# Seven down products of a SwiGLU layer, spread in another order over four tiles, with each product's weight sum fetched a tile earlier

## The chip, the cores and the metric

The program runs on one core of a Trainium2 chip. That core has a matrix engine (TensorE; PE in the profile, its weight loads PEld), a vector engine (VectorE, DVE), an activation engine (ScalarE, ACT), GpSimd (POOL) and a queue that issues transfers (SyncE, SP). Each engine runs its own list of instructions in order and waits on semaphores for the others. The metric is the device time of one launch in microseconds, as the median of several runs.

## The reference

One decoder layer on 512 tokens of width 1024: a SwiGLU block, a mixer (dilated attention and a gated recurrence), and a second SwiGLU block, each between RMS norms, all in float32:

```python
def swiglu(x, w_gate, w_up, w_down):
    return (jax.nn.silu(x @ w_gate) * (x @ w_up)) @ w_down

f = swiglu(rms_norm(h, ffn1_norm_pre), ffn1_w_gate, ffn1_w_up, ffn1_w_down)
h = h + 0.5 * rms_norm(f, ffn1_norm_post)
...  # the mixer
f = swiglu(rms_norm(h, ffn2_norm_pre), ffn2_w_gate, ffn2_w_up, ffn2_w_down)
h = h + 0.5 * rms_norm(f, ffn2_norm_post)
```

The hidden width is 2816, that is 22 tiles of 128. The change touches the two SwiGLU blocks alone ("first part" in its short description is the first group of four tiles of each block).

## The kernel before

**Number format.** A float32 operand is split into a high part (rounded by ACT, `split`, L260) and a low part (what is left, by DVE, L261); a product is three matmuls: high by high, high by low, low by high. "The form" of something below is this pair. Its high part is made on ACT, its low part on DVE, and TensorE needs both.

**One SwiGLU block** (`ffn`). Tiles 0 to 3 are computed by plain products (`gemm`, `std_out`). Tiles 4 to 21 go through `prod(f, w)`: gate and up of one tile as seven products p1 to p7 (a 2x2 split of the matrices) in place of eight. `w_forms` (L556) makes the seven weight forms of the next tile out of one 1 MB transfer (`raw`): sums on DVE, then four splits. Inside `prod` three results are copied out of PSUM in the middle of the tile: after p1 to a second bank (L793), after p5 (`copy`, L781) and after p6 (`copy`, L781). p6 and p7 accumulate onto the bank that was just copied, so TensorE can't start p6 before the copy after p1 and can't start p7 before the copy after p6.

**Down.** Tiles 0 to 15 are multiplied by the down matrix in four groups a = 0 to 3 of four tiles each, again as seven products, here called steps p1, p2, p5, p6, p7, p3, p4 (`step`, L735 to L760). A step is twelve matmuls of 128x512 (two token blocks of 128, two rows of the group, three matmuls each). It goes to one of two pairs of PSUM banks: p1, p6, p7 and p4 to `db` (banks 3 and 4), p2, p5 and p3 to `dz` (banks 6 and 7); a result that accumulates is read out to `facc` after every step (L756 by ACT, L758 and L760 by DVE). Tiles 16 to 21 are done at the end of the block by `last_product`.

**What a step needs.** (1) The forms of the activations, seven per group, made out of the four tiles' results in `ub` by `first_forms` (p1, p5) and `other_forms` (p2, p3, p6, p7, p4); they lie in `act`, one slot for each of the seven. (2) The form of its weight sum, in one of two buffers `wd0` and `wd1` used in turn: the form of a step can be made only when the step two before it is through. (3) The weight sum itself. The sums are made by transfers that add: in `npair` (`home.x`) u0 + u1 is the sum of p5, adding g0 makes that of p6, adding g1 that of p3; in `dr0` g0 is that of p1, and u0 + g0, loaded anew, that of p7; in `dr1` g1 is that of p2 and u1, loaded anew, that of p4. All these transfers stand in POOL's queue, in order. Adding to `npair` can start only when the form of the step before was read from it.

**The order before.** `ffn_order` puts a window of steps behind each `prod(f)`: in a steady group (p1, p2), (p5, p6), (p7, p3), (p4). `supply(a, p)` makes the form of a step and issues the next load; it is called for the step two ahead, with `tc.high_priority(offset=AHEAD)`. So p5 and p6 fall into one tile, and the form of p6 there waits for a transfer that can start only when the form of p5 is made. The final order on each engine is made by a scheduler out of program order, priorities and estimated durations, not by the program text alone.

```python
WINDOWS = (("p1", "p2"), ("p5", "p6"), ("p7", "p3"), ("p4",))
FIRST_WINDOWS = ((), ("p1", "p2"), ("p5", "p6"), ("p7", "p3", "p4"))
```

## Time and profile before

| | |
|---|---|
| median of 3 runs | 1268.39 us (1267.67 to 1268.49) |
| profiled execution | 1268.15 us, of which the span of the instructions is 1266.4 us |
| mean granted TensorE clock | 0.989 |
| busy: PE, PEld, DVE, ACT, POOL | 97%, 88%, 78%, 56%, 6% of the span |
| first SwiGLU block with its start | about 0 to 345 us |
| second SwiGLU block | from about 925 us on |

In the timeline a row is: start and duration in microseconds, engine, line and operation, result <- operands, and in brackets how long the engine had stood idle before it and what released it. In the windows view a row is a stretch of the span: its length, then each engine's busy time with its count of instructions, the granted TensorE clock (1.00 is full speed), the share of time the transfer engines were busy, and GB/s. In the waits view a row is: engine and line that waited <- engine and line it waited for: microseconds in total, times, longest.

### The profile page before, as it was taken

The numbers are of one execution on the slowest core, as the hardware profiler recorded it, in microseconds if no ns is written. First come the engines' busy times: TensorE is split into PE (matmuls) and PEld (weight loads), VectorE is DVE, ScalarE is ACT, GpSimd is POOL, SyncE is SP. The second block draws the span as 40 slices with busy tenths as digits, with TensorE's granted clock in tenths as the row PEclk, the third lists the DMA queues.
The fourth block names the chain that finished last, engine by engine and source line by source line (L and its number), as shares of the span: only waits on it lengthen the run. The fifth ranks groups of instructions, "written<-read, shape, count | busy, mean of one in ns | idle before, by whom it ended". The sixth has DMA issues, their size and how long they took to land. (4 is left out here: it accounts for less than half of the span.)

```text
span 1266.4 us, 19105 instructions
## 1 busy us (share of the span) xinstructions
PE 1228.6 (97%) x7652; PEld 1110.0 (88%) x7652; DVE 987.4 (78%) x1549; ACT 704.1 (56%) x1159; POOL 75.9 (6%) x123
## 2 busy tenths in 40 slices
PE   9899999989999999999999999999999999999997
PEld 7789898989977899999988787888899889898996
DVE  7989898988577488898665878655789788888855
ACT  7556454544455456656545978734656545555442
POOL 1001110100102000000000000000110111010000
PEclk9999999999999999999999999999999999999999
DMA  8246554543634222232242221325552555455241
GB/s 288 89 113 181 134 167 116 167 117 101 233 117 145 80 100 76 78 107 69 99 168 98 100 100 67 127 84 207 155 176 100 148 128 160 122 167 128 78 172 67
DMA packets 35449, 162.36 MB, mean 128 GB/s; under 512 B 3872, under 2 KB 7072, under 8 KB 23328
## 3 DMA queue, kind: packets, MB, share of 16 engines
q1 hardware_dynamic: 17712, 106.08, 23.0%
q0 software_dynamic: 17648, 55.06, 17.3%
q8 instruction: 60, 0.98, 0.3%
q14 instruction: 29, 0.24, 0.1%
HBM read 150.64 MB, written 6.29 MB: 124 GB/s over the span
## 5 line engine op out<-in xcount | busy, mean ns | idle before, releaser
L261 DVE TENSOR_TENSOR w<-raw,w 128x1024 fp32r<-128x1024 f32 (+1 forms) x241 | 257.8, 1073 | 88.7 <-ACT w L260 84.5
L260 ACT ACTIVATE w<-raw 128x1024 fp32r<-128x1024 f32 (+1 forms) x241 | 224.9, 938 | 132.2 <-PE bank L277 47.2
L774 PE MATMUL bank<-big,w 128*128 128x256 f32 x864 | 251.1, 291 | 21.1 <-ACT c L781 16.1
L776 PE MATMUL bank<-big,w 128*128 128x256 f32 x864 | 248.5, 288 | 1.5 <-DVE w L261 1.5
L775 PE MATMUL bank<-big,w 128*128 128x256 f32 x864 | 248.4, 288 | 0.0
L774 PEld LDWEIGHTS bank<-big,w 128*128 128x128 f32 x864 | 169.9, 197 | 26.9 <-ACT c L781 18.1
L776 PEld LDWEIGHTS bank<-big,w 128*128 128x128 f32 x864 | 169.6, 196 | 2.0 <-DVE w L261 1.9
L775 PEld LDWEIGHTS bank<-big,w 128*128 128x128 f32 x864 | 169.9, 197 | 1.4
L586 PE MATMUL bank<-big,w 128*128 128x256 f32 x320 | 92.0, 288 | 0.0
L587 PE MATMUL bank<-big,w 128*128 128x256 f32 x320 | 91.8, 287 | 0.0
L588 PE MATMUL bank<-big,w 128*128 128x256 f32 x320 | 91.0, 284 | 0.0
L745 PE MATMUL bank<-wd,act 128*128 128x512 f32 x224 | 87.7, 392 | 0.0
L744 PE MATMUL bank<-wd,act 128*128 128x512 f32 x224 | 87.1, 391 | 0.0
L746 PE MATMUL bank<-wd,act 128*128 128x512 f32 x224 | 87.0, 390 | 0.0
L261 DVE TENSOR_TENSOR w<-s,w 128x1024 fp32r<-128x1024 f32 x52 | 63.6, 1223 | 15.4 <-ACT w L260 15.2
L275 PE MATMUL bank<-big,w 128*128 128x512 f32 x192 | 74.8, 389 | 0.0
L277 PE MATMUL bank<-big,w 128*128 128x512 f32 x192 | 74.8, 389 | 0.0
L276 PE MATMUL bank<-big,w 128*128 128x512 f32 x192 | 74.7, 389 | 0.0
L586 PEld LDWEIGHTS bank<-big,w 128*128 128x128 f32 x320 | 61.3, 191 | 1.1
L587 PEld LDWEIGHTS bank<-big,w 128*128 128x128 f32 x320 | 61.3, 192 | 0.0
L588 PEld LDWEIGHTS bank<-big,w 128*128 128x128 f32 x320 | 61.3, 192 | 0.0
L260 ACT ACTIVATE w<-s 128x1024 fp32r<-128x1024 f32 x52 | 54.8, 1054 | 8.1 <-PE bank L588 5.4
(332 smaller groups left out, 2969.3 us busy)
## 6 DMA issues: line engine op xcount, KB each, us to landing
raw<-in_w SPq DMA_DIRECT2D x94, 1024.0 KB, 4.8
dr<-in_wdn POOLq DMA_DIRECT2D x40, 512.0 KB, 4.4
npair<-in_wdn POOLq DMA_DIRECT2D x32, 512.0 KB, 5.5
big<-act POOLq DMA_DIRECT2D x6, 512.0 KB, 4.6
h<-in_x SPq DMA_DIRECT2D x8, 256.0 KB, 6.0
h<-in_xn POOLq DMA_DIRECT2D x4, 512.0 KB, 5.5
kept_m<-h POOLq DMA_DIRECT2D x4, 512.0 KB, 2.9
h<-kept_m POOLq DMA_DIRECT2D x4, 512.0 KB, 4.8
```

The costliest lines, as they stand in the source:

```text
L260: ACT.activation(dh, src, AF.Copy)
L261: DVE.tensor_sub(dl, src, dh.bitcast(F32))
L275: PE.matmul(ps, wh, xh, start=first, stop=False)
L586: PE.matmul(ps, wh, xh, start=start and k == 0, stop=False, skip_group_check=True)
L587: PE.matmul(ps, wh, xl, start=False, stop=False, skip_group_check=True)
L588: PE.matmul(ps, wl, xh, start=False, stop=k == 3, skip_group_check=True)
L744: PE.matmul(ps, xh, wh, start=start and k == 0, stop=False, skip_group_check=True)
L745: PE.matmul(ps, xh, wl, start=False, stop=False, skip_group_check=True)
L746: PE.matmul(ps, xl, wh, start=False, stop=k == 1, skip_group_check=True)
L774: PE.matmul(ps, wh, xh, start=start and k == 0, stop=False, skip_group_check=True)
L775: PE.matmul(ps, wh, xl, start=False, stop=False, skip_group_check=True)
L776: PE.matmul(ps, wl, xh, start=False, stop=k == 3, skip_group_check=True)
```

## The change

- The windows are the same for all four groups: (p1, p2), (p5), (p6, p7), (p3, p4), and start one tile later: group a begins after tile 5 + 4a where it began after tile 4 + 4a (5 for the first group).
- The form of a step is no longer made two steps ahead by `supply` with raised priority, but inside `prod`, between its p2 and p7, for the steps that follow that tile. `down_form` then issues the transfer of the next step that uses the same tile of sums (`NEXT`).
- The activation forms are made in three portions, at tiles with f % 4 equal to 2 (p1, p5), 3 (p2, p6, p7, and the sum for p4) and 0 (p3, p4). Tile 4's result goes to a temporary, and ACT copies it to `ub` after the first group's forms.
- The first loads of a block (`begin`) no longer start as soon as the queue reaches them: two one-element DVE copies out of tile 1's result into `dr0` and `dr1` hold them back until that result exists; the loads of p5 follow after tile 3.
- The slots of `act` for tiles 16 to 21 and the spare room move by one tile.

```diff
-WINDOWS = (("p1", "p2"), ("p5", "p6"), ("p7", "p3"), ("p4",))
-FIRST_WINDOWS = ((), ("p1", "p2"), ("p5", "p6"), ("p7", "p3", "p4"))
+WINDOWS = (("p1", "p2"), ("p5",), ("p6", "p7"), ("p3", "p4"))
...
-        if f // 4 <= SEVEN:
-            a = f // 4 - 1
-            order.append(("window", a, (FIRST_WINDOWS if a == 0 else WINDOWS)[f % 4]))
+        a, i = divmod(f - NSTD - 1, 4)
+        if 0 <= a < SEVEN:
+            order.append(("window", a, WINDOWS[i]))
...
+        def second_forms():
             act_form("p2", x10)
+            DVE.tensor_sub(x01, x11, x01)
+            DVE.scalar_tensor_tensor(x00, x11, -1.0, x00, op0=ALU.mult, op1=ALU.subtract)
+            act_form("p6", x00)
+            act_form("p7", x01)
+
+        def third_forms():
+            DVE.scalar_tensor_tensor(x10, x00, -1.0, x10, op0=ALU.mult, op1=ALU.subtract)
+
+        def fourth_forms():
             act_form("p3", x11)
...
             act_form("p4", x10)
...
+        def supply(a, p):
+
+            if p in ("p5", "p6", "p3"):
+                dst, qs = home.x, {"p5": ("u0", "u1"), "p6": ("g0",), "p3": ("g1",)}[p]
+            else:
+                dst, qs = dr[p in ("p2", "p4")], {"p1": ("g0",), "p2": ("g1",), "p7": ("u0", "g0"), "p4": ("u1",)}[p]
+            for i, q in enumerate(qs):
+                load(dst, a, q, i > 0 or p in ("p6", "p3"))
+            at[p] = dst
+
+        NEXT = {"p1": "p7", "p2": "p4", "p5": "p6", "p6": "p3", "p7": "p1", "p3": "p5", "p4": "p2"}
+
+        def down_form(a, p):
             w = wdt[home.n % 2]
             home.n += 1
-            split(w[:, 0, :], w[:, 1, :], src)
+            split(w[:, 0, :], w[:, 1, :], at[p])
             ready[p] = w
-
-        def supply(a, p):
-
-            with tc.high_priority(offset=AHEAD):
...
+            q = NEXT[p]
+            a += p in ("p7", "p3", "p4")
+            if a < SEVEN:
+                supply(a, q)
+
+        def begin():
+            for i in range(2):
+                DVE.tensor_copy(dr[i][:, 0:1], ub[:, 1, 0:1])
+            for p in ("p1", "p2"):
+                supply(0, p)
...
-            u = ub[:, f % 4, :] if f < LAST[0] else tmp("u")
+            u = ub[:, f % 4, :] if NSTD < f < LAST[0] else tmp("u")
...
+            for a, p in due:
+                down_form(a, p)
             product("p7", b, False)
...
-            elif f % 4 == (2 if f < 8 else 1):
+                if f == LAST[0]:
+                    fourth_forms()
+            elif f % 4 == 2:
                 first_forms()
             elif f % 4 == 3:
-                other_forms()
+                second_forms()
+                third_forms()
+            elif f % 4 == 0 and f > NSTD:
+                fourth_forms()
...
+                if j == 1:
+                    begin()
                 if j + 1 == NSTD:
+                    supply(0, "p5")
...
-                u = prod(ev[1], forms.pop(ev[1]))
+                due = order[i + 1]
+                u = prod(ev[1], forms.pop(ev[1]), [(due[1], p) for p in due[2]] if due[0] == "window" else [])
                 if ev[1] == NSTD:
-                    for _ in range(2):
-                        supply(*todo.pop(0))
+                    first_forms()
+                    second_forms()
+                    third_forms()
+                    fourth_forms()
+                    ACT.activation(ub[:, 0, :], u, AF.Copy)
...
                     step(ev[1], p)
-                    if todo:
-                        supply(*todo.pop(0))
```

The counts of matmuls, splits and transfers stay as they are; two DVE copies of 128x1 and one ACT copy of 128x512 per block are added.

More of the change, by code (lines that the diff above doesn't have):

```diff
@@ L624, in __init__ @@
             self.x = npair.rearrange("p k t -> p (k t)")
-            self.n = 0
+            self.n = self.m = 0
         def slot(self, i):
@@ L637, in room @@
         def room(self):
-            return self.act[:, 12:16, :].rearrange("p (s k) t -> p s (k t)", s=2)
+            return self.act[:, 10:14, :].rearrange("p (s k) t -> p s (k t)", s=2)
         def gain_rows(self):
@@ L668, in ffn @@
         lo_, hi_ = HALVES
+        x00, x01, x10, x11 = ub[:, 0:2, lo_], ub[:, 0:2, hi_], ub[:, 2:4, lo_], ub[:, 2:4, hi_]
         def first_forms():
-            x00, x01 = ub[:, 0:2, lo_], ub[:, 0:2, hi_]
             act_form("p1", x00)
@@ L674, in first_forms @@
             act_form("p5", x00)
-        def other_forms():
-            d1, x01, x10, x11 = ub[:, 0:2, lo_], ub[:, 0:2, hi_], ub[:, 2:4, lo_], ub[:, 2:4, hi_]
+        def second_forms():
             act_form("p2", x10)
-            act_form("p3", x11)
-            DVE.tensor_sub(x01, x11, x01)
-            DVE.scalar_tensor_tensor(x11, x11, -1.0, d1, op0=ALU.mult, op1=ALU.subtract)
-            act_form("p6", x11)
-            act_form("p7", x01)
-            DVE.scalar_tensor_tensor(x10, x11, -1.0, x10, op0=ALU.mult, op1=ALU.subtract)
+            DVE.tensor_sub(x01, x11, x01)
[5 more added lines that the diff above has]
+        def fourth_forms():
+            act_form("p3", x11)
             act_form("p4", x10)
         def last_act(f):
-            v = home.slot(f - LAST[0])
+            v = home.slot((f - LAST[0] - 1) % 8)
             return v[:, 0, :], v[:, 1, :]
@@ L698, in load @@
                 nc.gpsimd.dma_start(dst, stored(a, q))
-        ready = {}
-        def down_form(p, src):
+        ready, at = {}, {}
+        def supply(a, p):
[8 more added lines that the diff above has]
+        def down_form(a, p):
             w = wdt[home.n % 2]
             home.n += 1
-            split(w[:, 0, :], w[:, 1, :], src)
+            split(w[:, 0, :], w[:, 1, :], at[p])
             ready[p] = w
-        def supply(a, p):
-            with tc.high_priority(offset=AHEAD):
-                if p == "p1":
-                    load(dr[0], a, "g0")
-                    down_form(p, dr[0])
-                    load(home.x, a, "u0")
-                    load(home.x, a, "u1", True)
-                elif p == "p2":
-                    load(dr[1], a, "g1")
-                    down_form(p, dr[1])
-                elif p == "p5":
-                    down_form(p, home.x)
-                    load(home.x, a, "g0", True)
-                    load(dr[0], a, "u0")
-                    load(dr[0], a, "g0", True)
-                elif p == "p6":
-                    down_form(p, home.x)
-                    load(home.x, a, "g1", True)
-                elif p == "p7":
-                    down_form(p, dr[0])
-                    load(dr[1], a, "u1")
-                elif p == "p3":
-                    down_form(p, home.x)
-                else:
-                    down_form(p, dr[1])
+            q = NEXT[p]
[7 more added lines that the diff above has]
+                supply(0, p)
         def step(a, p):
@@ L760, in step, with prod @@
                         DVE.tensor_add(y, ps, y)
-        def prod(f, w):
+        def prod(f, w, due):
             g = tmp("g")
             b, y, z = b_of[f % 2][:, :HB], y_[:, :HB], z_[:, :HB]
-            u = ub[:, f % 4, :] if f < LAST[0] else tmp("u")
+            u = ub[:, f % 4, :] if NSTD < f < LAST[0] else tmp("u")
             def product(p, ps, start):
@@ L817, in finish @@
                 split(*last_act(f), u)
-            elif f % 4 == (2 if f < 8 else 1):
+                if f == LAST[0]:
+                    fourth_forms()
+            elif f % 4 == 2:
                 first_forms()
             elif f % 4 == 3:
-                other_forms()
+                second_forms()
+                third_forms()
+            elif f % 4 == 0 and f > NSTD:
+                fourth_forms()
         keys = [(w, n, i) for i in range(NSTD) for w in ("gate", "up")]
         forms = {}
-        todo = [(a, p) for a in range(SEVEN) for p in STEPS]
-        for ev in ffn_order(n):
+        order = ffn_order(n)
+        for i, ev in enumerate(order):
             if ev[0] == "std":
@@ L834, in ffn @@
                     steps[j]()
+                if j == 1:
+                    begin()
                 if j + 1 == NSTD:
+                    supply(0, "p5")
                     for f in steps[NSTD:]:
                         f()
-                    first_forms()
-                    other_forms()
             elif ev[0] == "prep":
```

## The prediction

> **What bounds the kernel now.** First the page's busy line.

> ```profile
> span 1266.4 us, 19105 instructions
> PE 1228.6 (97%) x7652; PEld 1110.0 (88%) x7652; DVE 987.4 (78%) x1549; ACT 704.1 (56%) x1159; POOL 75.9 (6%) x123
> ```

> TensorE is busy for 1228.6 of 1266.4 us, and the change leaves its matmuls as they are. So it can gain only from the 37.8 us in which PE stands idle, or from stretches in which PE runs at a lower clock; it can lose by new idle time. Second, the waits view, for PE.

> ```profile
> PE bank L774 <- ACT c L781: 16.1, 7, 3.8
> PE bank L774 <- ACT big L260: 3.2, 1, 3.2
> ```

> The first entry is a product in `prod` that waits for ACT's copy `c`. Third, the timeline of PE, for where these waits lie.

> ```profile
> 57.68 0.39 PE L776 MATMUL bank<-big,w 128*128 128x256 f32 x1 [1.10 <-DVE w L261]
> 62.37 0.80 PE L774 MATMUL bank<-big,w 128*128 128x256 f32 x2 [3.23 <-ACT big L260]
> 95.67 0.38 PE L774 MATMUL bank<-big,w 128*128 128x256 f32 x1 [1.49 <-ACT c L781]
> 145.78 0.57 PE L774 MATMUL bank<-big,w 128*128 128x256 f32 x1 [2.02 <-ACT c L781]
> 209.31 0.39 PE L774 MATMUL bank<-big,w 128*128 128x256 f32 x1 [2.18 <-ACT c L781]
> 274.44 0.39 PE L774 MATMUL bank<-big,w 128*128 128x256 f32 x1 [3.77 <-ACT c L781]
> 989.71 0.39 PE L774 MATMUL bank<-big,w 128*128 128x256 f32 x1 [0.98 <-DVE ub L786]
> 1039.80 0.38 PE L774 MATMUL bank<-big,w 128*128 128x256 f32 x1 [2.37 <-ACT c L781]
> 1103.30 0.38 PE L774 MATMUL bank<-big,w 128*128 128x256 f32 x1 [2.15 <-ACT c L781]
> 1165.24 0.39 PE L774 MATMUL bank<-big,w 128*128 128x256 f32 x1 [2.07 <-ACT c L781]
> ```

> Six stalls of 2.0 to 3.8 us come once per group of four tiles, in groups 1 to 3 of both blocks; the 1.49 at 95.67 is the first group's. Their cause, around 209.31, in the timeline of ACT, DVE and POOL:

> ```profile
> 198.70 1.06 ACT L260 ACTIVATE wd<-npair 128x1024 fp32r<-128x1024 f32 x1 [1.64 <-PE bank L746]
> 200.67 1.22 DVE L261 TENSOR_TENSOR wd<-npair,wd 128x1024 fp32r<-128x1024 f32 x1
> 202.30 0.89 POOL L696 DMA_DIRECT2D npair<-in_wdn  x1 [13.10 <-DVE wd L261]
> 207.93 1.06 ACT L260 ACTIVATE wd<-npair 128x1024 fp32r<-128x1024 f32 x1 [3.26 <-DMA npair<-in_wdn]
> 208.90 0.37 ACT L781 ACTIVATE c<-bank 128x256 f32<-128x256 f32 x1
> ```

> p5's form is made at 198.70 and its low part on DVE at 200.67; only then POOL starts the transfer that adds to `npair`, and ACT stands 3.26 us before p6's form until it has landed. The copy `c` that frees p7's bank stands behind that form: it runs at 208.90, and PE goes on at 209.31. From form to form it takes 207.93 - 198.70 = 9.2 us, and one tile isn't long enough for both.

> Fourth, the windows view, by stretches from stall to stall and just behind two stalls; it shows the clock.

> ```profile
> 60.50:67.30 6.80, 4.93 (x23) 4.94 (x24) 5.87 (x7) 2.21 (x3) 0.86 (x2) 0.50 0.66 231
> 145.78:149.20 3.42, 3.42 (x16) 3.42 (x17) 2.62 (x4) 2.11 (x3) 0.87 (x1) 0.51 0.15 13
> 210.68:214.10 3.42, 3.42 (x18) 3.42 (x17) 2.59 (x4) 0.75 (x1) 0.86 (x1) 0.50 0.54 83
> 145.78:209.31 63.53, 61.35 (x420) 57.60 (x420) 55.83 (x81) 32.54 (x51) 6.24 (x9) 0.97 0.51 141
> 209.31:274.44 65.13, 61.35 (x421) 57.61 (x421) 56.49 (x82) 33.07 (x52) 6.20 (x9) 0.97 0.50 138
> 274.44:345.00 70.56, 70.56 (x477) 66.14 (x478) 50.69 (x70) 34.23 (x53) 5.50 (x9) 0.98 0.49 158
> 1039.80:1103.30 63.50, 61.35 (x420) 57.60 (x420) 55.84 (x81) 32.55 (x51) 6.19 (x9) 0.97 0.51 141
> 1103.30:1165.24 61.94, 59.87 (x421) 56.12 (x421) 56.32 (x82) 33.07 (x52) 6.22 (x9) 1.00 0.52 145
> 1165.24:1225.00 59.76, 59.76 (x427) 57.07 (x428) 44.84 (x62) 29.51 (x46) 3.54 (x6) 0.97 0.36 115
> ```

> The granted clock falls to half (0.50, 0.51) for 3.42 us behind the stalls of 2.02 and 2.18 us. Half of such a window is lost, 1.7 us. The whole stretches say where it happened: 0.97 of 63.5 us is 1.9 us short of full, so one window each; only 1103.30:1165.24 has 1.00. PE's work shows it too: about 420 matmuls took 61.35 us in the stretches with a window and 59.87 in the one without. So five of the six stalls bring a half-clock window. The stall of 3.23 at 62.37 lies in two (6.80 us at 0.50).

> [...]

> **The change, part by part.** The sum is made against the profiled execution (1268.15 us, span 1266.4), 0.24 under the median of 1268.39; I leave this difference aside.

> *p5 and p6 in different tiles.* In a steady group each form of `wd` is now made outside the stretch between the three copies: p5's early in the tile with f % 4 = 2, p6's at that tile's end, 8 to 9 us later (an estimate from the order of ACT's instructions with the durations above). The 9.2 us from form to form are just about there; if the transfer is late by a us, p6's form delays no copy that PE needs soon, as p6's first matmul follows only behind the next tile's products, some 10 us on or more (four tiles take 60 to 65 us in the rows above). p7, p3, p4, p1 and p2 have a tile or more each, and the additions still stand in POOL's queue in the order of their use. So all six stalls go: 2.02 + 2.18 + 3.77 + 2.37 + 2.15 + 2.07 = 14.56 us. With them go five windows of half clock: 5 x 1.7 = 8.5 us.

> *What is late next.* The cover of every step is DVE, which needs 55.8 to 56.5 us per four tiles; PE without stall and window needs 63.53 - 2.18 - 1.7 = 59.65. So DVE fits with 3 us to spare, less than it has now: between 1103.30 and 1165.24 it stood idle for 61.94 - 56.32 = 5.62 us. I cost it at nothing, since no instruction is added for it and what PE waited for was ACT; without the cover each us that it is late costs one per group.

> *Two steps behind one tile.* In (p1, p2), (p6, p7) and (p3, p4), ACT has a second form and a form of activations ahead of the copy out of the bank (L793). Now:

> ```profile
> 47.54 0.63 ACT L260 ACTIVATE act<-ub 128x512 fp32r<-128x512 f32 x1 [0.94 <-PE bank L277]
> ...
> 174.39 0.37 ACT L793 ACTIVATE bank<-bank 128x256 f32<-128x256 f32 x1 [0.39 <-PE bank L776]
> 175.77 0.38 ACT L781 ACTIVATE c<-bank 128x256 f32<-128x256 f32 x1 [1.01 <-PE bank L776]
> ```

> ACT stood 0.39 idle before that copy; a form of 0.63 ahead of it makes the copy 0.24 later. PE reaches the next copy's product 175.77 - 174.39 = 1.38 us on, less 0.37 for the copy: 1.0 us of slack, so it is hidden. p6 and p7 share banks 3 and 4, so the second begins only when the first was read out. I take 0.05 us in each of eight groups, 0.4; the bounds are 0 and the 0.3 per group of one read-out, 2.4.

> *The start of the first block.* The forms of p1 and p2 were made by 23.48, the second's start; the delayed loads put them behind `tx` on ACT, at 48.08:

> ```profile
> 23.48 1.05 ACT L260 ACTIVATE wd<-dr 128x1024 fp32r<-128x1024 f32 x1
> 42.98 1.22 DVE L472 TENSOR_TENSOR t<-h 128x1024 f32<-128x1024 f32 x1
> 48.08 1.05 ACT L260 ACTIVATE tx<-t 128x1024 fp32r<-128x1024 f32 x1
> 50.57 1.06 ACT L260 ACTIVATE big<-h 128x1024 fp32r<-128x1024 f32 x1 [1.45 <-DVE h L490]
> 52.43 1.06 ACT L260 ACTIVATE w<-s 128x1024 fp32r<-128x1024 f32 x1
> 53.52 1.23 DVE L261 TENSOR_TENSOR w<-s,w 128x1024 fp32r<-128x1024 f32 x1
> dr<-in_wdn POOLq DMA_DIRECT2D x40, 512.0 KB, 4.4
> ```

> The small DVE copies stand right behind the row at 42.98, so the loads start at about 44.5 and land 4.4 us later, at 49, the second at 50 (an estimate). Two forms are 2 x 1.06 = 2.1 us on ACT; 1.45 us of idle stand before 50.57, so `w` at 52.43 is 0.6 to 0.8 us later, and DVE's 53.52 with it. DVE has no idle time from there to the stall at 62.37, which grows by 0.8 (from 0, if the loads land early, to 2.1).

> The two stalls of the first group other than the 1.49 are these, in PE's timeline:

> ```profile
> 82.85 0.39 PE L776 MATMUL bank<-big,w 128*128 128x256 f32 x1 [0.39 <-DVE w L261]
> 85.58 0.39 PE L774 MATMUL bank<-big,w 128*128 128x256 f32 x1 [0.30 <-DVE ub L786]
> ```

> The first group is now drawn into four tiles like the others but its activation forms come only after tile 4, so p5's low form stands behind weight sums: I take the wait at 95.67 as 2.1 in place of 1.49 (+0.6), 0.9 for sums that DVE makes later, 0.7 for the copy behind the forms, and 0.7 off for these 0.39 and 0.30, which go with the order that made them. A stall of 2.1 also brings a window, +1.7. Together 0.8 + 0.6 + 0.9 + 0.7 - 0.7 + 1.7 = 4.0; bounds 0 (none comes) and 9 (the two forms in full, and 3.77, the largest stall there is, with its window on top of the present ones).

> *The second block's start.* ACT and DVE have idle time there, so the forms cost nothing. p6's form no longer stands ahead of the sums at 989.71: 0.98 becomes about 0.6, -0.4 (0 to -1). The copy of 128x512 (0.63 by the form of that size) and the small DVE copies are hidden, as is the moved spare room.

> Sum: -14.6 - 8.5 - 0.4 + 0.4 + 4.0 = -19.1. From 1268.15 that is 1249.0 us.

> **The rivals.**

> *DVE becomes the bound (slower).* The 5.6 us idle per group is time in which DVE waited in order for ACT's high parts and can't be worked off. Then four tiles go on taking about 62 to 65 us whatever ACT copies, the stalls only move from `c` to DVE's `w`, and the start's 4.0 is lost: 1272. It decides from 4 us of idle per group on, where 56.3 + 5.6 exceeds 59.65 by the 2.3 that a stall now costs. Against it: the stretch 274.44 to 345.00 has no stall with the same engines, and much of the present idle is caused by the stall itself.

> *The half clock isn't these stalls'.* If four of the five windows come from something else than the 2 us stalls, only the 3.77's window goes, and a new stall of 2.1 brings none: -14.6 - 1.7 - 0.4 + 0.4 + 2.3 gives 1254.1. Against it: 0.50 in 210.68:214.10, right behind a 2.18 stall. [...]

> *The copy out of the bank is late.* If the forms delay L793 by 0.7 us more than its slack in 14 tiles with two steps: +9.8, about 1259. Against it: 1.0 us of slack against 0.24.

> *The first block's start costs its upper bound:* up to +9, so 1253 to 1254, to 1260 if weights of the first group are late as well. For it: DVE has no idle time there.

> *It doesn't do what it says:* p6's form still waits between the copies, about 1268. Against it: in the built order it stands behind the tile's last copy.

> **How the numbers follow.** Main case (1243 to 1253) 0.64; better than 1243, with no cost at the start and shorter waits elsewhere, 0.03; clock rival 0.07; late copy 0.07; heavy start 0.07; no change 0.03; DVE bound 0.09. The time is the main case's, 1249.0. From 1242 to 1260 hold the main case, the clock, the copy and the start, 0.85; the start's bounds of 0 and +9 alone make 1245 to 1254. About 0.2% (2.5 us) is what a measurement tells from no change: faster 0.88, same 0.03, slower 0.09.

> **What would show it.** In the changed kernel's waits, PE behind ACT's `c` falls from 16.1 us to about 2, all at the first group; stretches of four tiles last 59.7 to 60.5 us at a clock of 1.00; the stall at 62 is 4.0 and the one at 57.68 1.1 to 1.9; p6's form waits for its transfer without PE waiting. It would be wrong if PE waits for DVE's `w` or `act` forms once a tile, for L793's copy, or if 0.50 stays without stalls.

## The result and the profile after

The changed kernel takes 1281.33 us (median of four runs, 1277.50 to 1282.36) against 1268.03 for the kernel before: a ratio of 1.0112, with a 95% interval of 1.0072 to 1.0152. It is slower by 1.1%, where 1249.0 was forecast with 1242 to 1260 as the range. The kernel before was run again beside every experiment, and moved by some tenths of a per cent from one set of runs to the next (medians of 1262.05 to 1268.39), so what follows goes by ratios.

The profiled execution of the changed kernel took 1281.76 us. First its page, the span and the busy line:

```profile
span 1280.0 us, 19095 instructions
PE 1234.2 (96%) x7652; PEld 1112.6 (87%) x7652; DVE 986.1 (77%) x1553; ACT 705.4 (55%) x1161; POOL 75.6 (6%) x123
```

The span grew by 13.6 us. PE stands idle for 45.8 us in place of 37.8, which is 8.0 of it; the other 5.6 are busy time of the same 7652 matmuls, that is, a lower clock (a mean of 0.984 where it was 0.989). Second, the waits of PE (who waited <- for whom: us, times, longest):

```profile
PE bank L772 <- ACT bank L791: 11.2, 6, 2.7
PE bank L772 <- DVE ub L784: 8.0, 5, 3.4
PE bank L772 <- DVE u L784: 3.6, 2, 2.1
PE bank L772 <- ACT big L259: 3.2, 1, 3.2
```

L772, L779, L784 and L791 are the lines 774, 781, 786 and 793 of before. The copy `c`, 16.1 us before, is no longer at the head: its stalls in the later groups are gone, as forecast. In their place stand 11.2 us behind the copy out of the bank (L791) and 11.6 behind the sums (L784), which had 1.8 before. In PE's timeline:

```profile
60.26 0.79 PE L772 MATMUL bank<-big,w 128*128 128x256 f32 x2 [3.24 <-ACT big L259]
114.14 1.22 PE L742 MATMUL bank<-wd,act 128*128 128x512 f32 x2 [2.63 <-ACT wd L259]
172.84 0.39 PE L772 MATMUL bank<-big,w 128*128 128x256 f32 x1 [0.97 <-DVE ub L784]
200.70 0.39 PE L772 MATMUL bank<-tx,w 128*128 128x256 f32 x1 [2.48 <-ACT bank L791]
238.30 0.39 PE L772 MATMUL bank<-big,w 128*128 128x256 f32 x1 [1.22 <-DVE ub L784]
265.55 0.38 PE L772 MATMUL bank<-tx,w 128*128 128x256 f32 x1 [1.75 <-ACT bank L791]
303.07 0.39 PE L772 MATMUL bank<-big,w 128*128 128x256 f32 x1 [1.53 <-DVE u L784]
...
1045.12 0.44 PE L772 MATMUL bank<-big,w 128*128 128x256 f32 x1 [3.40 <-DVE ub L784]
```

Two stalls come again and again. One is at the boundary of two groups, where p1's and p2's forms are made, ahead of groups 2 and 3: 2.48 and 1.75 here, 2.47 and 1.42 in the second block, 8.1 us together. The other follows p6's form, in groups 1, 2 and 3: 0.97, 1.22 and 1.53 here, 1.23, 1.22 and 2.06 in the second block, 8.2 us together.

**The stall at the boundary.** The timelines of ACT, DVE and POOL up to 200.70, in order of time:

```profile
180.27 1.04 ACT L259 ACTIVATE wd<-dr 128x1024 fp32r<-128x1024 f32 x1
183.58 1.22 DVE L260 TENSOR_TENSOR wd<-npair,wd 128x1024 fp32r<-128x1024 f32 x1
185.47 0.55 POOL L701 DMA_DIRECT2D npair<-in_wdn  x1 [14.06 <-ACT c L779]
189.06 1.22 DVE L260 TENSOR_TENSOR wd<-dr,wd 128x1024 fp32r<-128x1024 f32 x1
189.58 0.90 POOL L699 DMA_DIRECT2D npair<-in_wdn  x1 [3.57 <-DMA npair<-in_wdn]
190.89 0.55 POOL L701 DMA_DIRECT2D dr<-in_wdn  x1 [0.41 <-DVE ub L810]
199.32 1.06 ACT L259 ACTIVATE wd<-dr 128x1024 fp32r<-128x1024 f32 x1 [3.53 <-DMA dr<-in_wdn]
200.28 0.37 ACT L791 ACTIVATE bank<-bank 128x256 f32<-128x256 f32 x1
```

p3's form has its low part at 183.58, p4's only at 189.06, though ACT made its high part at 180.27. p5's two loads follow p3's form (185.47, 189.58), and the load of p2's sum follows p4's (190.89), behind them in the queue. It is used about a tile later, at 199.32, 8.3 us after its issue, where the median of such loads is 4.2: ACT waits 3.53 us for it, and the copy out of the bank stands behind this form as the copy `c` stood behind p6's form before.

**The stall behind p6's form.** The timelines of ACT, DVE and POOL up to 172.84, in order of time:

```profile
148.04 1.04 ACT L259 ACTIVATE wd<-npair 128x1024 fp32r<-128x1024 f32 x1
152.37 1.22 DVE L260 TENSOR_TENSOR wd<-npair,wd 128x1024 fp32r<-128x1024 f32 x1
154.26 0.85 POOL L699 DMA_DIRECT2D npair<-in_wdn  x1 [3.32 <-ACT c L779]
160.12 1.06 ACT L259 ACTIVATE wd<-npair 128x1024 fp32r<-128x1024 f32 x1 [2.81 <-DMA npair<-in_wdn]
161.21 1.23 DVE L260 TENSOR_TENSOR wd<-npair,wd 128x1024 fp32r<-128x1024 f32 x1 [1.93 <-ACT wd L259]
172.36 0.43 DVE L784 TENSOR_TENSOR ub<-bank,c 128x256 f32<-128x256 f32 x1
```

p5's form is made at 148.04, but its low part only at 152.37, and the transfer for p6 starts at 154.26. So p6's form still waits for its transfer, 2.81 us, now at the end of a tile where no copy stands behind it. But DVE's queue stands behind its low part for 1.93 us. DVE runs without a gap from there to 172.36, and the sum that frees the bank is late.

**A third wait** makes the stall at 1045.12. In the chain of work that ended last (start, us, what), and in DVE's timeline:

```profile
1026.20 10.86 DMA raw<-in_w
...
1037.08 0.69 DVE L561 TENSOR_TENSOR s<-raw 128x512 f32<-128x512 f32 x1 [4.89 <-DMA raw<-in_w]
```

The 1 MB transfer of the next tile's weights, 4.8 us by its median, was 10.86 us in coming, beside three loads of POOL's that were issued between 1021.85 and 1025.96. DVE waits 4.89 us for it.

### The profile page after: what moved, and what is told of

The parts are those of the page before. It is cut to its first block, busy times and chain, and to the rows that moved or that the text cites. A ratio compares the mean times of both kernels' runs of the same rounds, so it can differ in the third digit from the quotient of the medians.

```text
span 1280.0 us, 19095 instructions
## 1 busy us (share of the span) xinstructions
PE 1234.2 (96%) x7652; PEld 1112.6 (87%) x7652; DVE 986.1 (77%) x1553; ACT 705.4 (55%) x1161; POOL 75.6 (6%) x123
## 5 line engine op out<-in xcount | busy, mean ns | idle before, releaser
L260 DVE TENSOR_TENSOR w<-raw,w 128x1024 fp32r<-128x1024 f32 (+1 forms) x241 | 258.0, 1074 | 91.9 <-ACT w L259 87.8
L772 PE MATMUL bank<-big,w 128*128 128x256 f32 x864 | 250.2, 290 | 16.7 <-DVE ub L784 8.0
L774 PE MATMUL bank<-big,w 128*128 128x256 f32 x864 | 247.8, 287 | 1.4 <-DVE w L260 1.4
L772 PEld LDWEIGHTS bank<-big,w 128*128 128x128 f32 x864 | 169.0, 196 | 22.6 <-DVE ub L784 10.7
L774 PEld LDWEIGHTS bank<-big,w 128*128 128x128 f32 x864 | 169.1, 196 | 2.1 <-DVE w L260 1.9
L742 PE MATMUL bank<-wd,act 128*128 128x512 f32 x224 | 88.4, 399 | 2.6 <-ACT wd L259 2.6
L743 PE MATMUL bank<-wd,act 128*128 128x512 f32 x224 | 88.8, 397 | 0.0
L744 PE MATMUL bank<-wd,act 128*128 128x512 f32 x224 | 88.3, 394 | 0.0
L260 DVE TENSOR_TENSOR w<-s,w 128x1024 fp32r<-128x1024 f32 x52 | 63.6, 1224 | 22.0 <-ACT w L259 21.3
## 6 DMA issues: line engine op xcount, KB each, us to landing
dr<-in_wdn POOLq DMA_DIRECT2D x40, 512.0 KB, 4.2
npair<-in_wdn POOLq DMA_DIRECT2D x32, 512.0 KB, 5.5
big<-act POOLq DMA_DIRECT2D x6, 512.0 KB, 3.6
h<-in_xn POOLq DMA_DIRECT2D x4, 512.0 KB, 5.4
kept_m<-h POOLq DMA_DIRECT2D x4, 512.0 KB, 2.9
h<-kept_m POOLq DMA_DIRECT2D x4, 512.0 KB, 4.9
```

The source lines that it names most:

```text
L260: DVE.tensor_sub(dl, src, dh.bitcast(F32))
L742: PE.matmul(ps, xh, wh, start=start and k == 0, stop=False, skip_group_check=True)
L743: PE.matmul(ps, xh, wl, start=False, stop=False, skip_group_check=True)
L744: PE.matmul(ps, xl, wh, start=False, stop=k == 1, skip_group_check=True)
L772: PE.matmul(ps, wh, xh, start=start and k == 0, stop=False, skip_group_check=True)
L774: PE.matmul(ps, wl, xh, start=False, stop=k == 3, skip_group_check=True)
```

## The experiments

Edits are to the changed kernel where nothing else is said; "ratio" is the time over that of the kernel before, run beside it.

**p2's load first.** The loads of p5 are held until p4's form is made.

```diff
-            if a < SEVEN:
+            if a < SEVEN and q != "p5":
                 supply(a, q)
+            if a < SEVEN and q == "p2":
+                DVE.tensor_copy(home.x[:, 0:1], w[:, 1, 0:1].bitcast(F32))
+                supply(a, "p5")
```

> One edit to the changed kernel: the two loads of p5's sum are held until p4's form is made, so that the load of p2's sum stands ahead of them in POOL's queue. Theory (p2's sum lands late because p5's two loads lie ahead of it, and the copy out of the bank, L791, stands behind p2's form on ACT): p2's form no longer waits 3.5 us for its transfer, the four stalls at L791 of 2.48, 1.75, 2.47 and 1.42 us at the group boundaries go (8.1), and with them the two half-clock windows behind the first two (3.4): about 1270 us. Rival (DVE is the bound, so the time comes back as waits for the sums of L784): above 1278. Rival (p4's low part on DVE is so late that its place in POOL's queue doesn't matter): p2's form still waits over 2 us, about 1280.

Measured: 1275.07 us, ratio 1.0087 (1.0059 to 1.0115). None of the four stalls at the boundaries has a successor at the copy out of the bank; but four new ones of 2.25, 1.73, 3.24 and 1.52 us stand at the sums a tile later (8.7 us for the 8.1 that went). The place of the cause was right, and the gain was not (0.25% where 0.9% was expected): the wait moved on.

**Nothing holds the first loads.** The two one-element copies in `begin` are taken out.

```diff
-            for i in range(2):
-                DVE.tensor_copy(dr[i][:, 0:1], ub[:, 1, 0:1])
             for p in ("p1", "p2"):
```

> One edit to the changed kernel: the two one-element copies that hold back a block's first loads are taken out, so that these loads start as early as in the kernel before. Theory of the prediction (the hold puts p1's and p2's forms into a crowded stretch and costs up to 4 us): about 1277. Rival (the early loads take transfer time from the first weights; without them the first block came 2.1 us earlier to the stall at 57.68): about 1283 us, with that stall at 57.7 again instead of 55.6. The stalls at L791 and L784 of the later groups stay in both.

Measured: 1272.94 us, ratio 1.0072 (1.0039 to 1.0105), so 0.4% better than the changed kernel, with intervals that overlap. The stall of 55.56 comes at 59.72 (57.68 in the kernel before): the hold does save 4 us at the start. More than that goes later when the hold is out: 2.63 at 114.14 becomes 1.20, 2.75 at 1001.71 becomes 1.16, 1.68 at 962.57 goes.

**All forms at raised priority**, as the kernel before had them.

```diff
-            for a, p in due:
-                down_form(a, p)
+            with tc.high_priority(offset=AHEAD):
+                for a, p in due:
+                    down_form(a, p)
```

> One edit to the changed kernel: the forms of the weight sums are made with raised priority, as the kernel before made them. Theory (the low parts of p5's and p4's forms are 3 to 9 us late on DVE, so the transfers that wait for them start late): both transfers start 3 us or more earlier, the four L791 stalls (8.1 us, with 3.4 of clock) and the four of 1.0 to 1.2 at L784 (4.6) shrink by half at least: 1265 to 1274 us. Rival (DVE's order is full, and low parts made earlier push weight forms and sums later): waits of PE for DVE's w and for the sums grow, 1281 us or more.

Measured: 1259.51 us, ratio 0.9955 (0.9923 to 0.9987): this one edit takes 1.6% off, more than was expected, and makes the kernel faster than before. PE's waits in its trace:

```profile
PE bank L772 <- ACT c L779: 11.8, 7, 2.2
PE bank L772 <- ACT big L259: 3.2, 1, 3.2
PE bank L772 <- ACT bank L791: 2.5, 2, 2.2
```

Both kinds of stall are gone but for the first group. What is left is the old one: p6's form is made early again, and so between the copies.

```profile
202.89 1.04 ACT L259 ACTIVATE wd<-npair 128x1024 fp32r<-128x1024 f32 x1
211.74 1.06 ACT L259 ACTIVATE wd<-npair 128x1024 fp32r<-128x1024 f32 x1 [3.19 <-DMA npair<-in_wdn]
212.70 0.37 ACT L779 ACTIVATE c<-bank 128x256 f32<-128x256 f32 x1
213.12 0.39 PE L772 MATMUL bank<-big,w 128*128 128x256 f32 x1 [2.12 <-ACT c L779]
```

**p6's form without its transfer.** It is made from p5's sum as it stands, so p6 and p3 are other products.

```diff
-            for i, q in enumerate(qs):
+            for i, q in enumerate(qs if p != "p6" else ()):
```

> The changed kernel without the transfer that adds g0 to p5's sum: p6's form is made from p5's sum, so the products of p6 and p3 are other ones. Theory (p6's form still waits for this transfer, DVE stands in order behind its low part, and the sums of L784 a tile later are late by that): the stalls of 0.97, 1.22, 1.23 and 1.22 us at L784 in the later groups go (4.6), as do the first groups' 2.63 at L742 and 2.75 at L791 with two half-clock windows each (6.8): 1264 to 1268 us. Rival (DVE has too much work in the tiles of p6 and p7, whenever that form is made): the L784 stalls stay, and the time is above 1274.

Measured: 1260.73 us, ratio 0.997 (0.9943 to 0.9997). All six stalls behind p6's form are gone and so are those at 114.14 and 1001.71; those at the group boundary stay (2.23, 1.21, 3.27 and 1.48 at the copy out of the bank). DVE is busy for 985.9 us where it was 986.1, so its load did not make these stalls; the wait for this transfer did. The eight loads that are left out are also missing beside the others, so not all of the 1.4% need be the price of this wait.

**p6's form behind the SiLU.** All forms at raised priority, and p6's buffer is written to by a one-element ACT copy of the tile's last SiLU.

```diff
+            with tc.high_priority(offset=AHEAD):
                 for a, p in due:
                     down_form(a, p)
...
             ACT.activation(g[:, hi_], g[:, hi_], AF.Silu)
+            if due and due[0][1] == "p5":
+                ACT.activation(wdt[home.n % 2][:, 0, 0:1], g[:, T - 1:T], AF.Copy)
```

> The changed kernel with the forms at raised priority (as in the run before) and p6's form held behind the last SiLU of its tile by a one-element ACT copy into its buffer, so that it no longer stands between the copies c. Theory (the priority brings every transfer in time, and what is left there, five stalls of 1.9 to 2.2 us at the copy c, comes from p6's form alone, which again waits 3.2 us for its transfer between the copies): these 10.5 us go, and about 1247 us is left (1243 to 1251). Rival (a form that waits holds up whatever stands behind it: now the copy L791 or the sums L784): one wait of 1 to 2 us per group comes back there, 1255 us or more.

Measured: 1242.40 us, ratio 0.9852 (0.9831 to 0.9873), the fastest of all. Its busy line, the one stall of over 1 us left in the groups, and two stretches of 60 us in the windows view:

```profile
PE 1217.8 (98%) x7652; PEld 1101.0 (89%) x7652; DVE 984.2 (79%) x1553; ACT 707.4 (57%) x1169; POOL 75.6 (6%) x123
116.46 0.39 PE L772 MATMUL bank<-tx,w 128*128 128x256 f32 x1 [2.25 <-ACT bank L791]
140.00:200.00 60.00, 60.00 (x424) 56.49 (x423) 57.61 (x85) 33.58 (x52) 6.18 (x9) 1.00 0.56 162
1040.00:1100.00 60.00, 60.00 (x426) 56.43 (x425) 55.71 (x81) 33.29 (x52) 6.18 (x9) 1.00 0.53 150
```

PE is busy all the time at full clock, with DVE busy for 57.61 of 60 us beside it. That DVE is the bound falls with this.

**The kernel before with the windows and p6's form behind the SiLU**, and with nothing else of the change.

```diff
-WINDOWS = (("p1", "p2"), ("p5", "p6"), ("p7", "p3"), ("p4",))
+WINDOWS = (("p1", "p2"), ("p5",), ("p6", "p7"), ("p3", "p4"))
...
             ACT.activation(g[:, hi_], g[:, hi_], AF.Silu)
+            if f % 4 == 1 and 8 < f < 18:
+                ACT.activation(wdt[home.n % 2][:, 0, 0:1], g[:, T - 1:T], AF.Copy)
...
                     step(ev[1], p)
-                    if todo:
-                        supply(*todo.pop(0))
+                    for _ in range((0 if p == "p2" else 2 if p == "p5" else 1) if ev[1] else 1):
+                        if todo:
+                            supply(*todo.pop(0))
```

> The kernel before with three edits: the steady windows (p1, p2), (p5), (p6, p7), (p3, p4), p6's form supplied one step ahead and not two, and held behind the SiLU of the tile as above. First part, early loads, priorities and the order of the loads stay as they were. Theory (the six stalls at c came from p6's form between the copies, and the changed kernel lost its time by the other parts of the change): the six stalls of 14.6 us go, with whatever half clock they bring: 1243 to 1251 us. Rival (the windows themselves cost: two steps behind each of three tiles put forms ahead of the copies L793 and overload DVE): 1256 us or more, with new waits at L793 or L786.

Measured: 1246.79 us, ratio 0.9886 (0.9869 to 0.9903). All six stalls at `c` are gone and nothing takes their place.

**The kernel before with the windows alone** (the first two lines of the diff above).

> The kernel before with the steady windows (p1, p2), (p5), (p6, p7), (p3, p4) and nothing else: the forms are still made two steps ahead. Theory: p6's form still stands between the copies c and waits for its transfer, so the windows alone change nothing: 1260 to 1268 us, with six stalls of 2 us or more at c. Rival (the windows alone do it, since p5 and p6 lie in different tiles): 1250 us or less.

Measured: 1260.98 us, ratio 0.999 (0.9973 to 1.0008). Six stalls at `c` of 1.53 to 2.15 us remain: p6's form is made between the copies of p5's tile, whatever window p6 stands in.

**p6's form behind the SiLU, without the hold.**

This is the kernel of the run "p6's form behind the SiLU" (called the first of these four below), with the two copies in `begin` taken out.

> As the first of these four, and without the two copies that hold back the first loads. Theory (the hold saves about 4 us at the start of the kernel, and costs what the first groups wait in it, 2.2 and 0.8 us at raised priority): 0 to 2 us slower than the first of these four. Rival (the hold is a loss at raised priority as it was without, where it cost some 8 us): 4 us or more faster than the first of these four.

Measured: 1244.71 us, ratio 0.9871 (0.9851 to 0.9890), 0.19% or 2.3 us above the same kernel with the hold. The intervals overlap, so a small gain by the hold is likely and not shown; it is no longer a loss once the forms are early.

**Which forms count.** In four runs the priority is raised for some forms only; the diff is that of the run with p4, p1 and p2.

```diff
-            for a, p in due:
-                down_form(a, p)
+            for a, p in due:
+                with tc.high_priority(offset=AHEAD if p in ("p4", "p1", "p2") else 0):
+                    down_form(a, p)
```

p4 alone:

> The changed kernel with raised priority for p4's form alone: on DVE its low part now stands ahead of p3's, and in POOL's queue the load of p2's sum ahead of p5's two. Theory (p2's form waits for a load that starts late since p4's low part is late): the four stalls at L791 at the group boundaries go (8.1 us, with 3.4 of half clock), the four of 1.0 to 1.2 at L784 behind p6's form stay: 8 to 12 us off, a ratio to the kernel before of 1.002 to 1.005. Rival (the raised priority of p5's form did all of it): at most 3 us off, a ratio of 1.009 or more, with p2's form still waiting.

Measured: 1275.09 us, ratio 1.0099 (1.0072 to 1.0125): 0.1% and not 0.6 to 0.9% off. The boundary stalls went, as after the first edit, and as there new ones came a tile later. The timelines of POOL, DVE and PE show them:

```profile
199.94 0.54 POOL L701 DMA_DIRECT2D dr<-in_wdn  x1 [8.13 <-issue]
201.99 0.53 POOL L701 DMA_DIRECT2D dr<-in_wdn  x1 [1.50 <-DVE wd L260]
204.19 0.88 POOL L699 DMA_DIRECT2D dr<-in_wdn  x1 [1.68 <-DVE w L260]
215.04 0.69 DVE L561 TENSOR_TENSOR s<-raw 128x512 f32<-128x512 f32 x1 [4.30 <-DMA raw<-in_w]
223.26 0.58 PE L772 MATMUL bank<-big,w 128*128 128x256 f32 x1 [3.23 <-DVE ub L784]
```

Three loads follow p1's and p2's forms from 199.94 on, meet the weights' transfer, and DVE waits 4.30 us for it. p5 alone:

> The changed kernel with raised priority for p5's form alone, so that its low part is made 3 us or more earlier and the transfer for p6 starts earlier. Theory (p6's form holds up DVE since its transfer starts late): the stalls of 1.0 to 1.2 us at L784 go or turn into waits at the copy c (p6's form then comes between the copies again); the L791 stalls at the group boundaries stay: 0 to 6 us off, a ratio to the kernel before of 1.006 to 1.011. Rival (p5's low part is what all the stalls hang on): the L791 stalls go too, a ratio below 1.003.

Measured: 1278.68 us, ratio 1.0132 (1.0108 to 1.0157): no gain, outside the range on the slow side. In the group shown above, p5's low part ran at 152.56 and the transfer for p6 was issued at 154.21 (152.37 and 154.26 in the changed kernel), so the edit made neither earlier there, and the form waits 3.85 us. This run does not tell what p5's low part alone is worth. p4, p1 and p2:

> The changed kernel with raised priority for the forms of p4, p1 and p2. Theory (with p4's form alone the loads of p7's and p4's sums, which wait for the forms of p1 and p2, were issued in the time of the next 1 MB weight transfer, which then landed 3 to 4 us late; made earlier they are out of its way): the L784 and L791 stalls of 1.7 to 3.2 us once a group that the run with p4 alone had (9.9 us, with 3.4 of half clock) go, and those of 1.0 behind p6's form stay: a ratio to the kernel before of 0.996 to 1.003. Rival (p5's late low part holds these stalls): a ratio of 1.007 or more, with DVE still waiting 3 us or more for the weight transfer once a group.

Measured: 1256.13 us, ratio 0.9934 (0.9919 to 0.9949), a little better than expected. The three loads, and DVE's wait for the weights:

```profile
192.42 0.54 POOL L701 DMA_DIRECT2D dr<-in_wdn  x1 [4.10 <-DVE wd L260]
194.71 0.53 POOL L701 DMA_DIRECT2D dr<-in_wdn  x1 [1.74 <-DVE wd L260]
196.51 0.87 POOL L699 DMA_DIRECT2D dr<-in_wdn  x1 [1.27 <-DVE s L561]
207.38 0.69 DVE L561 TENSOR_TENSOR s<-raw 128x512 f32<-128x512 f32 x1 [0.96 <-DMA raw<-in_w]
```

They start 7.5 us earlier (2.7 of it because the whole group lies earlier, by p1's first matmul at 201.42 for 204.09), and the wait falls from 4.30 to 0.96. The six stalls behind p6's form stay, five of 1.0 to 1.3 and one of 1.85. p5 as well:

> The same with p5's form as well. Theory: p5's low part comes earlier, DVE no longer waits for p6's form, which slips between the copies c as with all forms raised: a ratio of 0.992 to 0.999, with five stalls of about 2 us at c. Rival (the forms of p6, p7 and p3 count too): above 1.000.

Measured: 1261.74 us, ratio 0.9978 (0.9967 to 0.9989), with five stalls of 2.02 to 2.31 at `c`. Raising p5's form costs 0.4%, since p6's form then slips between the copies. What the priority of p6, p7 and p3 does by itself was not tried.

## Why the prediction was wrong

The forecast lies 32.8 us below the profiled execution (1249.0 and 1281.76). Some 20 us of this are idle time of PE: the sum left 25.5 us (37.8 - 14.6 - 0.4 + 0.4 + 2.3), and 45.8 were measured. Some 12 us are half clock: ten windows where the sum left three, at 1.7 us each. The steps that failed are what a late transfer costs, the order of POOL's queue, and the dropped priority, which the sum put at nothing.

**p5 and p6 in different tiles.** Right in what it removes: the six stalls at `c` came from p6's form between the copies, and with that moved (and the windows, which alone gained nothing), the kernel before gained 1.1%. Wrong in the sentence on what a late transfer costs: "if the transfer is late by a us, p6's form delays no copy that PE needs soon". It looked at ACT's queue alone. The form is a pair, and DVE stood behind its low part for 1.93 us; the sums were late by 1.0 to 2.1 us in six groups. The run without the transfer shows it. The spacing was off as well: p6's form came 12.1 us after p5's (148.04 to 160.12) and not 8 to 9, since p5's low part ran 4.3 us behind its high part.

**The order of POOL's queue.** This step failed: "the additions still stand in POOL's queue in the order of their use". p2's load stood behind p5's two and was used first, and p7, p3, p4, p1 and p2 did not all have "a tile or more": from p4's low part (189.06) to p2's form (199.32) there were 10 us, in which p5's second load was issued ahead of p2's, and p2's took 8.3 us to land. The prediction took the spacing of the forms on ACT for the spacing of the transfers. A transfer starts behind the low part on DVE, and that was 9 us behind the high part (180.27 to 189.06). The order of the queue alone is not the whole price: with p2's load ahead, DVE waited 15.9 us in all for the next weights (L561, five waits), where it had waited 9.0 in four. That the weights come late beside POOL's loads (10.86 us at 1026.20, 4.8 by the median), the sum had nowhere.

**Why the low parts were late.** The change no longer raises the forms' priority. The description of the change had this, but no step of the sum costed it. Given back, it is worth 1.6% (1.0112 to 0.9955), and for p4, p1 and p2 alone 1.8% (to 0.9934). This overlaps with what p6's transfer costs (1.4% without it), so the two are not to be added.

**The late copy out of the bank.** The rival named the right line at 0.07, but by luck. Its reason was one more form of activations, 0.24 us against a slack of 1.0. The stalls there came from something else: a form that waits for its load ahead of the copy. For the 0.05 us a group that the sum took for two steps behind one tile, and for its bound of 0.3, no run shows a figure; a read-out took 0.59 us on ACT and 0.68 to 0.69 on DVE in the kernel before.

**DVE as the bound**, the rival on the slower side, was not the cause. The sums were late because DVE had waited, and p4's low part because the order of DVE's work put it late (DVE has no idle time between 180.27 and 189.06), not because there was too much work: DVE is busy for 57.61 us of 60 in the fastest kernel, with no stall.

**The start of the first block.** The stall at 62.37 did not grow: it came 2.1 us earlier, with the same 3.24 us. The prediction counted the two forms that the hold moves there but not what goes from the first 20 us: without the early loads PE's 1.08 us at 9.68 is gone, and with the hold taken out a stall of 2.13 is at 10.40. The first group had its 2.63 at 114.14, near the 2.1 that was forecast, but by luck: the forecast meant a wait for the copy `c`, and this is p6's transfer again, since it is gone without it.

**The second block's start** was costed at a gain of 0.4. It lost 1.68 at 962.57 and 2.75 at 1001.71. The former lies behind a wait of DVE for the weights, 2.55 us at 960.29. The latter is p6's transfer again: its form waits 3.51 us for it at 993.73, and the stall is gone without it.

**The clock.** Seven half-clock windows of 3.41 us became ten, where the sum left the two at the start and one new. That the stalls of 2 us bring them was right, but not as firmly as the sum had it: with all forms raised, the 2.12 at 213.12 brought none, and the mean clock of that execution, with six stalls of 1.92 to 2.23 us, was 0.996. The section below shows how the idle time of such stalls lay. The 8.5 us that the sum took off for five windows were therefore those of one execution: it had a mean clock of 0.989, and the thirteen of the same kernel beside the run of 1246.79 us had 0.990 to 0.995. There the kernel with the six stalls gone was 15.3 us faster, not the 23.1 (14.6 + 8.5) of the sum.

## What to carry to other kernels

When forms, copies and transfers share in-order queues, follow a moved step through every queue in which it has a part: here the low part on DVE starts the next transfer, and it was 9 us behind the part that was looked at. A wait that is moved away from one short critical copy holds up what stands behind it next; take away its cause (an earlier start of the transfer) or put it where nothing is due, and here both together gave 1.5%. Raised priority that a change drops is a part of the change, and is to be costed as one.

## What the runs showed of the hardware

```profile
142.41:145.82 3.41, 1.39 (x13) 1.19 (x11) 0.38 (x2) 1.42 (x3) 0.00 (x0) 1.00 0.40 79
145.82:149.23 3.41, 3.41 (x16) 3.41 (x17) 2.61 (x4) 2.07 (x3) 0.87 (x1) 0.50 0.15 13
1101.56:1104.97 3.41, 1.67 (x14) 1.67 (x15) 1.96 (x2) 3.05 (x5) 0.30 (x1) 1.00 0.00 0
1104.97:1108.38 3.41, 3.41 (x28) 3.32 (x27) 2.93 (x6) 1.28 (x3) 0.56 (x1) 1.00 0.59 84
```

2.02 us idle in one cell were followed by a clock of 0.50 in the next. Of the 2.15 at 1103.30 only 1.74 lie in one cell, and the clock stays at 1.00. The changed kernel's 2.47 at 1104.62 is cut in two, 1.19 and 1.28, and the clock stays at 1.00 as well:

```profile
1099.92:1103.34 3.42, 2.23 (x19) 2.02 (x17) 3.42 (x6) 0.10 (x1) 0.00 (x0) 1.00 0.52 180
1103.34:1106.75 3.41, 2.13 (x17) 2.13 (x18) 2.03 (x3) 1.92 (x5) 1.07 (x2) 1.00 0.46 148
1106.75:1110.16 3.41, 3.41 (x31) 3.41 (x30) 2.22 (x2) 2.27 (x3) 0.87 (x1) 1.00 0.79 183
```

In the two blocks of these two traces, up to 1250 us, thirteen cells at full clock had 1.75 to 3.22 us idle, and each was followed by half clock; none with 1.74 or less was. The nearest two are 0.01 us apart (1.75 at 263.66 in the changed kernel, 1.74 at 1101.56 in the kernel before), so a sharp limit is not shown. In a cell that was at half clock already, less was enough: 0.67 and 0.76 us (at 113.47 and 1000.94 in the changed kernel) and 1.40 and 1.87 (at 58.86 there and at 60.49 in the kernel before) were followed by a second half-clock cell, and the thirteen half-clock cells without idle time by full clock. So by these rows a stall of 2 us cost 2.0 or 3.7 us (with half of 3.41) by where it fell. The order of the work alone doesn't set that: the thirteen executions of the kernel before that are named above had mean clocks of 0.990 to 0.995.

The other thing not expected: a 1 MB load of SP's took long where it was issued within 0.3 us of the last of three 0.5 MB loads from POOL's queue. From issue to landing it took 10.9 us in the changed kernel (issued at 1026.20) and 11.0 with p4 alone raised (issued at 204.0), and DVE waited 4.89 and 4.30 us for it. It took 6.0 us in the changed kernel at 207.7, 4 us after POOL's loads of the same steps, and 4.8 by its median. Where POOL's three loads come earlier, with p4, p1 and p2 raised, DVE waited 0.96. So weights that DVE waited for came late beside POOL's loads; that the one held up the other is the author's reading, and by what means, these traces don't show.
